# Seven products of halves for both feed-forward output projections of a hybrid attention and mLSTM model

## The chip, the cores and the metric

The kernel runs on one core of a Trainium2 chip. The metric is the device time of one execution in microseconds (us); the median of three runs is compared. A core has TensorE for matmuls (PE in the profile; PEld is its weight load), VectorE (DVE), ScalarE (ACT), GpSimd (POOL) and SyncE (SP), which issues most DMAs here. Matmuls write into PSUM, eight banks of 128 x 512 float32; the other operands lie in SBUF.

## The reference

Two layers over 512 tokens of width 1024, in float32: attention and a feed-forward, then an mLSTM and a feed-forward, then a last norm.

```python
h = x
for i in range(DEPTH):                      # 2
    if i % N_MIXERS == 0:
        h = h + dilated_attention_mixer(rms_norm(h, attn_norm[j]), ...)
    else:
        h = h + mlstm_mixer(rms_norm(h, mlstm_norm[j]), ...)
    h = h + swiglu(rms_norm(h, ffn_norm[i]), ffn_w_in[i], ffn_w_out[i])
return rms_norm(h, final_norm)

def swiglu(xn, w_in, w_out):                # D_FF = 2816
    gu = xn @ w_in
    return (silu(gu[..., :D_FF]) * gu[..., D_FF:]) @ w_out
```

The change concerns the last product, `hidden @ w_out`: 512 x 2816 by 2816 x 1024, once in each layer. The 2816 rows are 22 row tiles of 128.

## The kernel before

**Precision.** A float32 product is made of three matmuls in a faster 32-bit format (`SPLITS`): each operand is split into a high part (ACT copies it with rounding) and a low part (DVE subtracts the high part from the original), and high x high, high x low and low x high are summed in PSUM. `load_chunk` brings 512 KB of weights with SP into a ring of three buffers (`wraw`), `split_chunk` makes the parts in two further rings of three (`whi`, `wlo`). So a split runs at most two chunks ahead of PE.

**Order.** The code's order is a priority, not the order of execution: a planner in the framework fixes each engine's order ahead of time, by its own costs, and takes the first instruction in code order that is ready by its reckoning. So line 1561, far down in the mLSTM's code, runs on DVE at 845.38, among the norm that stands ahead of it. At run time each engine follows its fixed order and waits on semaphores. `defer(n, fn)` traces a function only n chunks of a projection later (`advance` counts them).

**Feed-forward input (`ffn_in`).** The hidden features come in pairs of row tiles, eleven tiles `hid[0..10]` of 128 x 2 x 512. The first six row tiles (`PLAIN`) are plain products; the rest are made in blocks of two as seven products of halves (the Strassen-Winograd scheme: `PRODUCTS`), with sums of weight halves and sums of token halves (T1 to T4) made on DVE. Each product is 24 matmuls of 256 columns. `prepare` splits the weights of the product two ahead.

**First layer's output projection.** `split_hidden` makes high and low parts of all of hid; then four `project` calls (tiles `fo`, matmuls in line 239) multiply feature-major: weights stationary, tokens moving, 512 columns. DVE adds the result to h in an order that interleaves the tokens (line 1287). Then `norm("mlstm", ...)`: high and low halves of h (lines 226, 227), squares (1007), sums of squares added up (1008), and, deferred by one chunk, a product with ones (1015) that gives each token's sum, a Newton root on DVE, diagonal tiles (323), and a product that broadcasts the result (329, `hook`). The mLSTM begins with `project_tokens_wide`, line 297: four chunks of two row tiles each, with the gates' product after the second.

**Second layer's output projection.** Token-major (tiles `fin`, line 1620): tokens stationary, weights moving. The two halves of the features are made one after the other, eight chunks, then three chunks tile by tile, so that the result tiles end in turn. h is transposed on PE (32 transposes, `residual`) and added; ACT squares the sum (1639), POOL multiplies it by the gain (1644), a short chain on small tiles gives the scale (1648 to 1655), ACT and DVE scale the halves, and they go out. The last tile is cut into two of 256 columns.

**The same scheme elsewhere.** The attention values are already made in seven products with 512 moving columns, and their weight sums are partly made by the DMA: a load issued from POOL with `accum_op=ALU.add` (line 606) adds to what lies in SBUF.

Of the kernel before, what the change touches and what calls it, by code (L numbers as in the profile page):

```python
# [17 lines left out]
P = 128  # L18
# [53 lines left out]
def tile_hybrid_dilated_attn_mlstm(  # L72
# [925 lines left out]
    def norm(key, k0, name):  # L998
# [21 lines left out]
        defer(1, sums)  # L1020
# [7 lines left out]
    def ffn_in(layer, fp, pair, rbc, hook, following):  # L1028
# [208 lines left out]
        out_weights = []  # L1237

        def prepare(n):
            if n < len(todo):  # L1240
                j, i = todo[n]
                if j not in prepared:
                    prepared[j] = weights_of(j)
                prepared[j][0][i]()
            else:
                out_weights.append(following(n - len(todo)))


        parts = [], []

        def split_hidden():
            i = len(parts[0])
            hi = fp.tile([P, 2, SEQ], F32R, tag="op%d" % (i + 1 if i else 0), name="f%dhh%d" % (layer, i))
            nc.scalar.activation(hi, hid[i], AF.Copy)
            lo = (place(i - 1, "hl", F32R) if i else
                  fp.tile([P, 2, SEQ], F32R, tag="op1", name="f%dhl" % layer))
            nc.vector.tensor_tensor(lo, hid[i], hi.bitcast(F32), op=ALU.subtract)  # L1257
            for part, x in zip(parts, (hi, lo)):
                part.append(x)
# [3 lines left out]
        for n, (j, i) in enumerate(todo):  # L1263
            prepare(n + AHEAD)
            if i == 0:
                steps_of = products(j, prepared[j][1])
            steps_of[i]()
            if i % 2:
                advance()
            if n >= len(todo) - 3:  # L1270
                split_hidden()
        while len(parts[0]) < len(hid):
            split_hidden()
        return [[tiles[k // 2][:, k % 2] for k in range(FC)] for tiles in parts], out_weights

    pair, rbc, _, hook = norm("ffn", 0, "n1")
    with ExitStack() as fctx:
        fp = pool(fctx, "ffn0")
        a, ready = ffn_in(0, fp, pair, rbc, hook,
                          lambda ch: split_chunk(weight_chunk(ffn_w_out[0], ch, 0, 4, "fo0_k%d" % ch)))  # L1280

        old, h = h, []

        def natural(c):
            def evac(m, acc):
                t = hp.tile([P, SEQ], F32, tag="h", name="hn%d" % (2 * c + m), bufs=KC + 1)
                nc.vector.tensor_tensor(t.rearrange("p (j c) -> p c j", c=4),
                                        acc.rearrange("p (c j) -> p c j", c=4),
                                        old[2 * c + m].rearrange("p (c j) -> p c j", c=4), op=ALU.add)
                h.append(t)  # L1290
            return evac
        for c in range(KC // 2):
            project(a, ffn_w_out[0], c * 256, FC, natural(c), "fo%d" % c, ready=ready)


    pair, rbc, rtok, hook = norm("mlstm", 0, "n2")
# [280 lines left out]
    with ExitStack() as fctx:  # L1577
# [3 lines left out]
        def load(ch, n):  # L1581
            src = wo[ch * 2 * P:(ch + 1) * 2 * P, n * 512:(n + 1) * 512].rearrange("(k p) n -> p k n", p=P)
            return split_weights(src, [P, 2, 512], "fw%d_%d" % (n, ch))
        a, ready = ffn_in(1, fp, pair, rbc, hook, lambda ch: load(ch, 0))
        gbc = fp.tile([P, D], F32, tag="t1", name="gbc")
        nc.gpsimd.dma_start(gbc, final_norm.unsqueeze(0).to_broadcast([P, D]))

        ht = [[None, None] for _ in range(TB)]
        ht_tiles = [fp.tile([P, 4, SEQ], F32, tag="w8", name="ht%d" % i, bufs=2) for i in range(2)]

        def residual(i):
            tb, n = i // 2, i % 2
            tp = ps.tile([P, 512], F32, tag="so"[i % 2], name="hT%d" % i, bufs=2)
            for k in range(4):
                transpose_into(tp, k, h[4 * n + k][:, tb * P:(tb + 1) * P])
            t = ht_tiles[i // 4][:, i % 4]
            nc.scalar.activation(t, tp, AF.Copy)
            ht[tb][n] = t
        NCH = FC // 2
        fss = fp.tile([P, TB, 3], F32, name="fss")  # L1600
        fpre, fv, fr, fa = (fp.tile([P, TB], F32, name="f" + n) for n in ("pre", "v", "r", "a"))
        nc.gpsimd.memset(fss, 0.0)
        nc.gpsimd.tensor_scalar(gbc, gbc, -0.5, None, op0=ALU.mult)
        tail = 3
        for n in range(2):
            acc = ([acc_tile("fin%d" % i) for i in range(3)] + [ps.tile([P, 512], F32, tag="t", name="fin3", bufs=1)]
                   if n == 0 else
                   [ps.tile([P, 512], F32, tag=tg, name="fin4", bufs=2) for tg in ("s", "s", "o", "o")]
                   + [acc_tile("fin5")])


            tiles = [(tb, tb, slice(0, 512)) for tb in range(TB)]
            if n == 1:
                tiles[-1:] = [(TB - 1, TB - 1, slice(0, 256)), (TB, TB - 1, slice(256, 512))]

            def mm(whl, ch, i, tb, cs):
                for k in range(2):
                    kk = 2 * ch + k
                    for a_, b_ in SPLITS:
                        nc.tensor.matmul(acc[i][:, cs], a[a_][kk][:, tb * P:(tb + 1) * P], whl[b_][:, k, cs],  # L1620
                                         start=(kk == 0 and (a_, b_) == SPLITS[0]),
                                         stop=(kk == FC - 1 and (a_, b_) == SPLITS[-1]))

            for ch in range(NCH - tail):
                whl = ready.pop(0) if ready else load(ch, n)
                for t in tiles:
                    mm(whl, ch, *t)
                if n == 0 and 1 <= ch <= TB:
                    residual(2 * ch - 2)
                    residual(2 * ch - 1)  # L1630
            last = [load(ch, n) for ch in range(NCH - tail, NCH)]
            for at, tb, cs in tiles:
                for i in range(tail):
                    mm(last[i], NCH - tail + i, at, tb, cs)
                t = ht[tb][n][:, cs]
                nc.vector.tensor_tensor(t, acc[at][:, cs], t, op=ALU.add)
                junk = npl.tile([P, SEQ], F32, tag="sq", name="fsq", bufs=2)
                part = 0 if n == 0 else 1 if cs.stop < 512 else 2
                nc.scalar.activation(junk[:, cs], t, AF.Square, accum_out=fss[:, tb, part:part + 1])
                if part == (1 if tb == TB - 1 else 0):  # L1640
                    nc.vector.tensor_tensor(fpre[:, tb:tb + 1], fss[:, tb, 0:1], fss[:, tb, 1:2], op=ALU.add)
                    nc.vector.tensor_scalar(fpre[:, tb:tb + 1], fpre[:, tb:tb + 1], 1.0 / D, EPS,
                                            op0=ALU.mult, op1=ALU.add)
                nc.gpsimd.tensor_tensor(t, t, gbc[:, n * 512 + cs.start:n * 512 + cs.stop], op=ALU.mult)
                if n == 1 and cs.stop == 512:

                    v = fv[:, tb:tb + 1]
# [37 lines left out]
```

## Time and profile before

| what | value |
|---|---|
| median of three runs | 1433.47 us (1430.98 to 1434.05) |
| profiled execution, its own time | 1431.08 us |
| its span, mean granted clock | 1428.8 us, 0.997 |
| PE busy | 1410.0 us, 7968 matmuls |
| DVE, ACT, POOL busy | 988.5, 621.3, 78.1 us |
| first output projection, first matmul to the first of the next stage | 724.98 to 844.69 us |
| second output projection, first to last matmul's start | 1294.51 to 1418.77 us |

Times in the profile count from the span's start. Busy time of PE overlaps from one matmul to the next, so a stage on PE is read from starts, not from durations. In rows of the profile an instruction stands with its line, the tile that it writes, the tiles that it reads and its shape; the name behind `<-` in brackets is what ended the idle time before it.

### The profile page before, as it was taken

How to read it: one execution, taken by the hardware profiler on the slowest of the kernel's cores; microseconds unless marked ns; L12 is line 12 of the kernel's file. 1: busy time of each engine (PE TensorE's matmuls, PEld its weight loads, DVE VectorE, ACT ScalarE, POOL GpSimd, SP SyncE). 2: the span in 40 equal slices, each digit the busy share in tenths (PEclk: the TensorE clock that was granted, in tenths of full speed). 3: DMA queues.
4: the chain of work that ended last, by engine and by line, in shares of the span. 5: the costliest groups of instructions: out<-in, count | busy, mean ns of one | idle time of the engine just before them, and what ended most of it. 6: DMA issues, size and time to landing. Idle time of an engine off the chain costs nothing. (4 is left out here: it accounts for less than half of the span.)

```text
span 1428.8 us, 20252 instructions
## 1 busy us (share of the span) xinstructions
PE 1410.0 (99%) x7968; PEld 1234.9 (86%) x7968; DVE 988.5 (69%) x1697; ACT 621.3 (43%) x1027; POOL 78.1 (5%) x131
## 2 busy tenths in 40 slices
PE   9999999999999999999999999999999999999997
PEld 7788888888888888999988888798888899998886
DVE  7976685966676587777863359987759777786223
ACT  7245522324224443454542234785544344555222
POOL 1014010100001000000000010100000000000101
PEclk9999999999999999999999999999999999999998
DMA  9538353363525333332233333221233233313231
GB/s 297 144 86 210 96 167 121 99 211 98 176 89 165 108 95 111 119 118 80 70 111 97 103 91 89 75 75 50 84 102 101 93 118 119 105 59 119 74 118 59
DMA packets 132182, 160.74 MB, mean 112 GB/s; under 512 B 7092, under 2 KB 112884, under 8 KB 132088
## 3 DMA queue, kind: packets, MB, share of 16 engines
q1 hardware_dynamic: 123696, 135.75, 30.7%
q0 software_dynamic: 6736, 22.59, 6.1%
q8 instruction: 62, 1.02, 0.3%
q10 hardware_dynamic: 1656, 1.12, 0.2%
q14 instruction: 32, 0.26, 0.1%
HBM read 145.28 MB, written 12.06 MB: 110 GB/s over the span
## 5 line engine op out<-in xcount | busy, mean ns | idle before, releaser
L1620 PE MATMUL fin<-fw_h,f1hh 128*128 128x512 f32 (+1 forms) x198 | 72.8, 368 | 0.0
L1620 PE MATMUL fin<-fw_l,f1hh 128*128 128x512 f32 (+1 forms) x198 | 72.5, 366 | 0.0
L1620 PE MATMUL fin<-fw_h,f1hl 128*128 128x512 f32 (+1 forms) x198 | 72.4, 366 | 0.0
L209 DVE TENSOR_TENSOR fw_l<-fw_w,fw_h 128x1024 fp32r<-128x1024 f32 x22 | 27.0, 1233 | 65.5 <-ACT fw_h L208 65.5
L209 DVE TENSOR_TENSOR fo_k_l<-fo_k_w,fo_k_h 128x1024 fp32r<-128x1024 f32 (+1 forms) x24 | 27.2, 1133 | 62.0 <-ACT fo_k_h L208 62.0
L239 PE MATMUL fo<-f0hh,fo_k_h 128*128 128x512 f32 x176 | 68.5, 389 | 0.0
L239 PE MATMUL fo<-f0hl,fo_k_h 128*128 128x512 f32 x176 | 68.5, 389 | 0.0
L239 PE MATMUL fo<-f0hh,fo_k_l 128*128 128x512 f32 x176 | 68.5, 389 | 0.0
L208 ACT ACTIVATE fo_k_h<-fo_k_w 128x1024 fp32r<-128x1024 f32 (+1 forms) x24 | 23.7, 989 | 74.4 <-PE fo L239 74.4
L208 ACT ACTIVATE fw_h<-fw_w 128x1024 fp32r<-128x1024 f32 x22 | 23.3, 1059 | 67.8 <-PE fin L1620 67.8
L1620 PEld LDWEIGHTS fin<-fw_h,f1hl 128*128 128x128 f32 x198 | 37.3, 189 | 6.1
L1620 PEld LDWEIGHTS fin<-fw_l,f1hh 128*128 128x128 f32 x198 | 37.4, 189 | 6.0 <-DVE fw_l L209 0.2
L1620 PEld LDWEIGHTS fin<-fw_h,f1hh 128*128 128x128 f32 x198 | 37.4, 189 | 6.0
L239 PEld LDWEIGHTS fo<-f0hh,fo_k_h 128*128 128x128 f32 x176 | 33.0, 188 | 6.9
L239 PEld LDWEIGHTS fo<-f0hl,fo_k_h 128*128 128x128 f32 x176 | 33.0, 188 | 6.9
L239 PEld LDWEIGHTS fo<-f0hh,fo_k_l 128*128 128x128 f32 x176 | 33.0, 188 | 6.7
L239 PE MATMUL f1j<-n_h,f1j_h 128*128 128x512 f32 x96 | 37.5, 390 | 0.0
L239 PE MATMUL f0j<-n_h,f0j_h 128*128 128x512 f32 x96 | 37.5, 390 | 0.0
L239 PE MATMUL f0j<-n_h,f0j_l 128*128 128x512 f32 x96 | 37.4, 389 | 0.0
L239 PE MATMUL f1j<-n_h,f1j_l 128*128 128x512 f32 x96 | 37.4, 389 | 0.0
L239 PE MATMUL f0j<-n_l,f0j_h 128*128 128x512 f32 x96 | 37.3, 389 | 0.0
L239 PE MATMUL f1j<-n_l,f1j_h 128*128 128x512 f32 x96 | 37.3, 389 | 0.0
(2127 smaller groups left out, 4896.8 us busy)
## 6 DMA issues: line engine op xcount, KB each, us to landing
f0j_w<-in_ffn_w_in_dram SPq DMA_DIRECT2D x28, 512.0 KB, 4.8
f1j_w<-in_ffn_w_in_dram SPq DMA_DIRECT2D x28, 512.0 KB, 3.6
fw_w<-in_ffn_w_out_dram SPq DMA_DIRECT2D x22, 512.0 KB, 3.9
fo_k_w<-in_ffn_w_out_dram SPq DMA_DIRECT2D x20, 512.0 KB, 3.4
awo_k_w<-in_attn_w_out_dram SPq DMA_DIRECT2D x8, 512.0 KB, 4.5
mv_k_w<-in_mlstm_w_in_dram SPq DMA_DIRECT2D x8, 512.0 KB, 3.6
mqk_k_w<-in_mlstm_w_in_dram SPq DMA_DIRECT2D x8, 512.0 KB, 3.8
mo_k_w<-in_mlstm_w_in_dram SPq DMA_DIRECT2D x8, 512.0 KB, 3.6
```

The lines of the kernel that those rows point to most:

```text
L208: nc.scalar.activation(hi[:, :n], raw[:, :n], AF.Copy)
L209: nc.vector.tensor_tensor(lo[:, :n], raw[:, :n], hi[:, :n].bitcast(F32), op=ALU.subtract)
L239: nc.tensor.matmul(acc, whl[a][:, k, m * P:(m + 1) * P], pairs[b][kk], start=(kk == 0 and (a, b) == SPLITS[0]), stop=(kk == nk - 1 and (a, ...
L1620: nc.tensor.matmul(acc[i][:, cs], a[a_][kk][:, tb * P:(tb + 1) * P], whl[b_][:, k, cs], start=(kk == 0 and (a_, b_) == SPLITS[0]), stop=(k ...
```

## The change

Sixteen of the 22 row tiles, as a matrix of 2 x 2 halves (rows 0 to 1023 and 1024 to 2047, columns 0 to 511 and 512 to 1023; tokens 0 to 255 and 256 to 511), become one unit of seven products; the last six row tiles stay plain. Class `Halves` runs it as 34 items in the order of `HALF_ORDER`: a11 (items 0 to 3), a12 (4 to 7), plain steps for the first half of the features p0 (8 to 10), s1 (11 to 14), s2 (15 to 18), p1 (19 to 21), s3 (22 to 25), s4 (26 to 29), a22 (30 to 33). A product's item has two row tiles of weights, 512 columns. Weight sums lie in four tiles "own" (a21 + a22; then, with a11 added on DVE, for s2; then with a12, for s4) and four tiles "first" (a11, then a11 + a21, for s3). What a load can add is added by accumulating DMAs from POOL; DVE adds four times. Token forms: B11 and B21 from `hid`, sums T1 to T4 made in place in `hid`, B22; their high and low parts lie in three slots of op tiles, written anew as products end (`HALF_SLOT`). Results lie in pairs of PSUM banks: c (a11, a12), u (a copy of a11's result, then s2, s3, a22), p (s1, s4); they are folded into h, or into the result tile, after each product.

In the first layer weights stay stationary and 256 tokens move; h is reordered afterwards by ACT (`natural`). In the second layer tokens are stationary and 512 weight columns move. The mLSTM's norm defers its sums by two chunks. `split_hidden` and the old projections go.

```diff
-    def norm(key, k0, name):
+    def norm(key, k0, name, wait=1):
...
-        defer(1, sums)
+        defer(wait, sums)
...
-        def split_hidden():
...
+            unit.early(n - len(todo) + len(PRODUCTS))
+
+    HALF_ORDER = (("a11", "B11"), ("a12", "B21"), ("p0", None), ("s1", "T1"), ("s2", "T2"), ("p1", None),
+                  ("s3", "T3"), ("s4", "B22"), ("a22", "T4"))
+    HALF_SLOT = {"B11": 0, "B21": 1, "T1": 2, "T2": 0, "T3": 1, "B22": 2, "T4": 0}
+
+    class Halves:
...
+        def load(self, to, col, ch, add=False):
+            view = to.rearrange("p (k n) -> p k n", k=2)
+            if add:
+                nc.gpsimd.dma_start(view, self.source(col, ch), accum_op=ALU.add)
+            else:
+                nc.sync.dma_start(view, self.source(col, ch))
+
+        def load_own(self, c):
+            p, tag = (self.fp, ("op12", "op13", "t1")[c]) if c < 3 else (xp, "x7")
+            self.own[c] = p.tile([P, 1024], F32, tag=tag, name="o%down%d" % (self.layer, c))
+            self.load(self.own[c], 1, c)
+            self.load(self.own[c], 1, 4 + c, True)
...
+        def prepare(self, n):
...
+            if place:
+                raw = wp.tile([P, 1024], F32, tag="wraw", name=nm + "_w", bufs=W_BUFS)
+                self.load(raw, place[0], place[1] + c)
+            else:
+                raw = self.first[c // 2][:, c % 2] if key == "s3" else self.own[c]
+            self.made[n] = split_chunk((raw, 1024, lambda t: t.rearrange("p (k n) -> p k n", k=2), nm))
+            if key == "s2":
+                self.load(self.own[c], 0, 4 + c, True)
+            if n + 2 < len(self.items) and self.items[n + 2][0] == "s2":
+                c2 = self.items[n + 2][2]
+                first = self.first[c2 // 2][:, c2 % 2]
+                nc.vector.tensor_tensor(self.own[c2], self.own[c2], first, op=ALU.add)
+                self.load(first, 1, c2, True)
...
+        EARLY = {2: (("B11", 0),), 3: (("B11", 1),), 4: (("B11", 2),), 5: (("B11", 3),), 6: (("B21", 0), ("B21", 1))}
+        STEPS = {0: (("B21", 2),), 1: (("B21", 3), ("plain", 8)), 2: (("plain", 9),), 3: (("plain", 10),),
+                 4: (("T1", 0),), 5: (("T1", 1),), 6: (("T1", 2),), 7: (("T1", 3),),
+                 8: (("T2", 0), ("T2", 1)), 9: (("T2", 2), ("T2", 3)), 10: (("T3", 0),), 11: (("T3", 1),),
+                 13: (("T3", 2),), 15: (("T3", 3),), 16: (("B22", 0),), 17: (("B22", 1),),
+                 19: (("B22", 2), ("B22", 3)), 20: (("T4", 0), ("T4", 1)), 21: (("T4", 2), ("T4", 3))}
...
+            for n, (key, okey, c) in enumerate(self.items):
+                self.prepare(n + 2)
+                if n < 4:
+                    self.load_own(n) if n < 3 else None
+                elif n == 4:
+                    self.load_own(3)
+                if 5 <= n < 9:
+                    self.load_first(n - 5)
+                for what, i in self.STEPS.get(n, ()):
+                    self.step(what, i)
...
+        def mul(dst, m, okey, c, whl, first, last):
+            for k in range(2):
+                for a, b in SPLITS:
+                    nc.tensor.matmul(dst[m // 2][:, (m % 2) * HALF:(m % 2 + 1) * HALF], whl[a][:, k, m * P:(m + 1) * P],
+                                     unit.form(okey, b, 2 * c + k),
...
+                whole[n] = [unit.bank(*b) for b in ((("acc", 3), ("t", 1), ("s", 2), ("s", 2)),
+                                                    (("acc", 3), ("acc", 3), ("acc", 3), ("t", 1)))[n]]
...
+        def natural(f):
+            t = hp.tile([P, SEQ], F32, tag="h", name="hn%d" % f, bufs=KC + 1)
+            nc.scalar.activation(t.rearrange("p (j c) -> p c j", c=4), h[f].rearrange("p (c j) -> p c j", c=4), AF.Copy)
+            h[f] = t
...
+    pair, rbc, rtok, hook = norm("mlstm", 0, "n2", 2)
...
+        def finish(tb, n):
+            t = ht[tb][n]
+            junk = npl.tile([P, SEQ], F32, tag="sq", name="fsq", bufs=2)
+            nc.scalar.activation(junk, t, AF.Square, accum_out=fss[:, tb, n:n + 1])
+            nc.gpsimd.tensor_tensor(t, t, gbc[n], op=ALU.mult)
...
+        def mul(dst, t, okey, c, whl, first, last):
+            for k in range(2):
+                for a, b in SPLITS:
+                    nc.tensor.matmul(dst[t], unit.form(okey, a, 2 * c + k)[:, t * P:(t + 1) * P], whl[b][:, k],
...
+        def after(banks, key, t):
+            if key == "s1":
+                fold(2 + t, 1, banks["p"][t], ALU.subtract)
+            elif key == "s2":
+                fold(2 + t, 0, banks["u"][t])
+            elif key == "s3":
+                fold(2 + t, 1, banks["u"][t], ALU.subtract)
+                finish(2 + t, 1)
+            elif key == "s4":
+                fold(2 + t, 0, banks["p"][t])
+                finish(2 + t, 0)
+            elif key == "a22":
+                fold(t, 1, banks["u"][t], ALU.subtract)
+                finish(t, 1)
+        unit.run((2, mul, mul_plain, after), also)
```

More of the change, by code (lines that the diff above doesn't have):

```diff
@@ L1245, in prepare @@
             else:
-                out_weights.append(following(n - len(todo)))
-        parts = [], []
-        def split_hidden():
[L1252 to L1259, printed above, removed]
+                unit.prepare(n - len(todo))
         for n in range(AHEAD):
@@ L1292, in tile_hybrid_dilated_attn_mlstm @@
-        for c in range(KC // 2):
-            project(a, ffn_w_out[0], c * 256, FC, natural(c), "fo%d" % c, ready=ready)
-    pair, rbc, rtok, hook = norm("mlstm", 0, "n2")
+        unit = Halves(0, fp, ffn_w_out[0])
+        ffn_in(0, fp, pair, rbc, hook, unit)
+        whole = {}
+        def mul(dst, m, okey, c, whl, first, last):
[3 more added lines that the diff above has]
+                                     unit.form(okey, b, 2 * c + k),
+                                     start=(first and m % 2 == 0 and k == 0 and (a, b) == SPLITS[0]),
+                                     stop=(last and m % 2 == 1 and k == 1 and (a, b) == SPLITS[-1]), skip_group_check=True)
@@ new lines, in mul_plain @@
+        def mul_plain(banks, key, c, whl, fresh, last):
+            n = int(key[1])
+            if fresh:
+                whole[n] = [unit.bank(*b) for b in ((("acc", 3), ("t", 1), ("s", 2), ("s", 2)),
+                                                    (("acc", 3), ("acc", 3), ("acc", 3), ("t", 1)))[n]]
+            for m in range(4):
+                for k in range(2):
+                    for a, b in SPLITS:
+                        nc.tensor.matmul(whole[n][m], whl[a][:, k, m * P:(m + 1) * P], unit.plain[c][b][k],
+                                         start=(fresh and k == 0 and (a, b) == SPLITS[0]),
+                                         stop=(last and k == 1 and (a, b) == SPLITS[-1]))
+                if last:
+                    f = 4 * n + m
+                    nc.vector.tensor_tensor(h[f], whole[n][m], h[f], op=ALU.add)
+                    if n == 0:
+                        fold(banks["c"], m, f, 0, ALU.add)
@@ L1297, in tile_hybrid_dilated_attn_mlstm @@
+        unit.run((4, mul, mul_plain, after))
+    pair, rbc, rtok, hook = norm("mlstm", 0, "n2", 2)
     w_in2 = mlstm_w_in[0]
@@ L1579, in tile_hybrid_dilated_attn_mlstm @@
         wo = ffn_w_out[1]
[L1581 to L1586, printed above, removed]
+        unit = Halves(1, fp, wo)
+        ffn_in(1, fp, pair, rbc, hook, unit)
@@ L1597, in residual, with gains_in @@
             nc.scalar.activation(t, tp, AF.Copy)
-            ht[tb][n] = t
-        NCH = FC // 2
-        fss = fp.tile([P, TB, 3], F32, name="fss")
+        def gains_in():
+            for n in range(2):
+                t = hp.tile([P, SEQ], F32, tag="h", name="gbc%d" % n, bufs=KC + 1)
+                nc.gpsimd.dma_start(t, final_norm[n * 512:(n + 1) * 512].unsqueeze(0).to_broadcast([P, 512]))
+                nc.gpsimd.tensor_scalar(t, t, -0.5, None, op0=ALU.mult)
+                gbc.append(t)
@@ L1601, in tile_hybrid_dilated_attn_mlstm, with also @@
+        def also(n):
+            if n < 4:
+                for i in (2 * n, 2 * n + 1):
+                    residual(i % TB, i // TB)
+            elif n == 6:
+                gains_in()
+        fss = fp.tile([P, TB, 2], F32, name="fss")
         fpre, fv, fr, fa = (fp.tile([P, TB], F32, name="f" + n) for n in ("pre", "v", "r", "a"))
         nc.gpsimd.memset(fss, 0.0)
[L1603 to L1616, printed above, removed]
-                for k in range(2):
[L1618 to L1647, printed above, removed]
-                    nc.vector.scalar_tensor_tensor(v, fss[:, tb, 2:3], 1.0 / D, fpre[:, tb:tb + 1],
-                                                   op0=ALU.mult, op1=ALU.add)
-                    r = fr[:, tb:tb + 1]
-                    a2 = fa[:, tb:tb + 1]
-                    nc.scalar.activation(r, v, AF.Sqrt)
-                    nc.vector.reciprocal(r, r)
-                    nc.vector.tensor_scalar(a2, r, v, r, op0=ALU.mult, op1=ALU.mult)
-                    nc.vector.scalar_tensor_tensor(r, a2, -3.0, r, op0=ALU.add, op1=ALU.mult)
-                    t0, t1 = ht[tb]
-                    nc.scalar.activation(t0, t0, AF.Copy, scale=r)
-                    nc.scalar.dma_start(out[tb * P:(tb + 1) * P, 0:512], t0)
-                    nc.vector.tensor_scalar(t1, t1, r, None, op0=ALU.mult)
-                    nc.sync.dma_start(out[tb * P:(tb + 1) * P, 512:1024], t1)
```

181 lines of the change are left out of this document (158 added, 23 removed).

## The prediction

> **What bounds the kernel now.** I read the page's busy shares first, then busy time by stage, then the matmuls' starts at the borders of the stages that change.
>
> ```profile
> span 1428.8 us, 20252 instructions
> ...
> PE 1410.0 (99%) x7968; PEld 1234.9 (86%) x7968; DVE 988.5 (69%) x1697; ACT 621.3 (43%) x1027; POOL 78.1 (5%) x131
> ```
>
> TensorE is busy for 99% of the span. The same by stage (columns: length; busy time and count of PE, PEld, DVE, ACT, POOL; clock; DMA share; GB/s):
>
> ```profile
> 100.00:110.00 10.00, 10.00 (x46) 8.24 (x45) 6.05 (x6) 4.83 (x6) 1.47 (x3) 1.00 0.80 227
> 563.00:725.00 162.00, 162.00 (x1349) 161.85 (x1348) 128.81 (x124) 86.73 (x105) 0.00 (x0) 1.00 0.30 93
> 725.00:845.00 120.00, 120.00 (x532) 99.39 (x531) 47.95 (x50) 33.39 (x39) 0.31 (x1) 1.00 0.32 100
> 905.00:915.00 10.00, 8.20 (x37) 6.26 (x36) 9.67 (x16) 7.56 (x23) 1.04 (x2) 1.00 0.00 0
> 1294.00:1419.00 125.00, 125.00 (x632) 106.24 (x630) 42.96 (x60) 37.22 (x54) 9.92 (x8) 1.00 0.28 89
> ```
>
> The second and third rows are the first layer's feed-forward input and output, the last one the second layer's output projection. In all three PE is busy from end to end at full clock, so an output projection is worth what its matmuls take, one start after another. The second row matters most for what follows: there DVE carries 128.81 of 162.00 us, and PE loses nothing. The fourth row, early in the mLSTM stage, is the counterexample: DVE at 9.67 of 10 us, and PE lost 1.8.
>
> A matmul's busy time overlaps its neighbours', so its price is the distance between starts:
>
> ```profile
> 699.90 0.28 PE L1186 MATMUL f0j_p<-f0B22l,f0j18S_h 128*128 128x256 f32 x1
> 700.02 0.28 PE L1186 MATMUL f0j_p<-f0B22h,f0j18S_l 128*128 128x256 f32 x1
> ...
> 724.98 0.40 PE L239 MATMUL fo<-f0hh,fo_k_h 128*128 128x512 f32 x1
> ...
> 844.69 0.39 PE L297 MATMUL mv<-mv_k_h,n_h 128*128 128x512 f32 x1
> ...
> 1294.51 0.40 PE L1620 MATMUL fin<-fw_h,f1hh 128*128 128x512 f32 x1
> ```
>
> With 256 moving columns (the input's seven products) starts are 0.12 us apart. The first output projection runs from 724.98 to 844.69, 119.71 us for 3 x 176 = 528 matmuls of 512 columns: 0.2267 each. Two matmuls of 256 cost 0.24: halving the moving side loses 6%.
>
> ```profile
> L1620 PE MATMUL fin<-fw_h,f1hh 128*128 128x512 f32 x154 | 60.4, 392 | 0.0
> ...
> L209 DVE TENSOR_TENSOR fw_l<-fw_w,fw_h 128x1024 fp32r<-128x1024 f32 x22 | 27.0, 1233 | 65.5 <-ACT fw_h L208 65.5
> ...
> L1620 PE MATMUL fin<-fw_h,f1hh 128*128 128x256 f32 x44 | 12.4, 282 | 0.0
> ```
>
> These three rows, of the second output projection, give three kinds of matmul each: 462 of 512 columns and 132 of 256. It runs from 1294.51 to 1418.77 + 0.12 = 1418.89 (that start is quoted with the tail below): 124.4 us. 462 x 0.2267 + 132 x 0.12 = 120.6; the 3.8 left are its 32 transposes.
>
> **The matmuls after.** Sixteen of 22 row tiles become seven products of halves (8 row tiles, 256 tokens, 512 features), the other six stay plain.
> First projection, feature-major: 7 x 4 feature tiles x 8 row tiles x 3 = 672 matmuls of 256 columns, 80.6 us, and 8 x 6 x 3 = 144 of 512, 32.6 us: 113.3 against 119.7, so -6.4.
> Second, token-major: 7 x 2 token tiles x 8 x 3 = 336 of 512 columns, plus the same 144: 480 x 0.2267 = 108.8, with the transposes 112.6 against 124.4: -11.8. It gains more since it keeps 512 columns, and its last tile is no longer split.
> Together -18.2 us.
> [...]
>
> **VectorE.** By the weight-split row (1.23 us for 1024 columns) and 0.69 for 512 and 0.42 for 256 (tail rows below), a unit costs: 34 weight splits 41.8; 28 low halves of token forms 19.3; 16 sums of forms 11.0; 4 weight sums 4.9; three plain tiles 3.7; folds 15.6 in the first unit (8 x 0.69, 24 x 0.42) and 12.4 in the second (18 x 0.69). That is 96.3 and 93.1; six forms and two splits (6.6) are done in the last input products. So 90 of 113 us and 87 of 113, against 47.95 and 42.96 now (eleven token splits and 24 or 22 weight splits go), and near the 80% of the second quoted row. The average is covered; the peak is items 8 to 14 (last plain step of the first half, both sum products). There DVE has 29.4 us of work in the first unit (7 splits 8.6, 4 sums 4.9, three T3 forms 4.1, four T2 forms 5.5, folds 4.4 + 1.7) against 3 x 5.44 + 4 x 2.88 = 27.8 of PE. Two splits stand ahead of PE in the three-deep ring. If DVE keeps the written order, the excess of 1.6 and seven waits for ACT's high half (0.63 each, the 512-column ACT row below) make up to 6.0 us of stall. But the order is a planner's, which takes what is ready: T1 forms need only slots freed in the last input products, T2 forms only B11's, free after item 3. With T2 ahead the peak is 23.9, and nothing waits. Bounds per unit 0 and 6; I take 1.0, nearer to the second quoted row than to the fourth: +2.0 for both.
>
> **PSUM.** s1 in the first unit takes the two banks that the last plain step fills last. It waits for one add of 0.69 after the third tile, and the fourth tile's matmuls (1.36) cover that: 0, at most the folds ahead of it on DVE, inside the 6 above. The copy of a11 into the u banks (0.63) has half an item, 1.4, of cover.
>
> **GpSimd and DMA.** Per unit 38 loads of 512 KB, 19.9 MB in 113 us, is 176 GB/s; now it is 100 and 89. The attention values, which run the same seven products with the same accumulating loads, reach 227 at a share of 0.80 with PE at 10.00 of 10 (first row above). All twelve accumulations go through POOL's queue, behind loads on SP's. "first" and the third "own" tile lie where buffers free up during the input products (share 0.30); the first two "own" tiles must wait for the last one, the fourth for the last plain split. The first user of "own" is prepared eight products later, over 20 us. I cost this at 0; if that cover is gone it is the third rival. In the second unit POOL also multiplies eight result tiles by the gain while DVE works:
>
> ```profile
> 1284.85 3.04 POOL L1603 TENSOR_SCALAR gbc<-gbc 128x1024 f32<-128x1024 f32 x1 [3.24 <-DMA gbc<-in_final_norm_dram]
> ...
> 1285.16 2.06 DVE L209 TENSOR_TENSOR f1j20S_l<-f1j20A,f1j20S_h 128x1024 fp32r<-128x1024 f32 x1
> ```
>
> A DVE subtraction beside a POOL instruction took 2.06 instead of 1.23: +0.83. Two such multiplies fall into the peak: 1.7 us of DVE work, inside the bounds.
> [...]
>
> **The mLSTM's start.** Feature tiles 4 to 7 of h now end with the last item, and the norm's sums are put off by two chunks instead of one.
>
> ```profile
> 850.13 0.95 PE L1015 MATMUL n2ss<-ones,n2ssum 128*128 128x1 f32 x8
> ...
> 851.11 0.16 DVE L1017 COPY n2v<-n2ss 128x4 f32<-128x4 f32 x1 [0.32 <-PE n2ss L1015]
> ...
> 854.99 1.66 DVE L323 TENSOR_SCALAR n2dg<-cst,n2rhl 128x128 fp32r<-128x128 f32 x8
> ```
>
> Now the sums run 5.44 us after the first mLSTM matmul (844.69), the statistics reach DVE 0.98 later, and the diagonal tiles are done at 856.65, 5.54 after that. After: sums at 10.88, statistics at 11.86, tiles at 16.2 to 17.4 (without or with the weight split that sits among them); PE, through sums (0.8) and 16 gate matmuls (3.6), is ready for them at 15.3. So PE, and the gate chain on DVE, lose 0.9 to 2.1: I take 1.5. The lower bound is 0, if PE runs the next chunk first; the upper one is a rival. The high and low halves of tiles 0 to 3 are ready before the last item, those of 4 to 7 are needed 10.9 us later: 0. ACT's reordering copy of h has no row here; between the plain 0.63 and twice that, eight of them take 5 to 10 us, spread over the last eight items.
>
> **The tail.** The last matmul feeds a fold, a square, a short chain and a scaling:
>
> ```profile
> 1414.78 0.69 DVE L1636 TENSOR_TENSOR ht<-fin,ht 128x512 f32<-128x512 f32 x1 [0.51 <-PE fin L1620]
> ...
> 1415.50 0.63 ACT L1639 ACTIVATE fsq<-ht 128x512 f32<-128x512 f32 x1 [1.01 <-DVE ht L1636]
> ...
> 1416.31 1.30 POOL L1644 TENSOR_TENSOR ht<-ht,gbc 128x512 f32<-128x512 f32 x1 [2.65 <-ACT fsq L1639]
> ...
> 1418.77 0.28 PE L1620 MATMUL fin<-fw_h,f1hl 128*128 128x256 f32 x1
> 1419.09 0.42 DVE L1636 TENSOR_TENSOR ht<-fin,ht 128x256 f32<-128x256 f32 x1 [0.62 <-PE fin L1620]
> 1419.55 0.42 ACT L1639 ACTIVATE fsq<-ht 128x256 f32<-128x256 f32 x1 [0.89 <-DVE ht L1636]
> ...
> 1421.28 0.72 ACT L1657 ACTIVATE ht<-ht,fr 128x512 f32<-128x512 f32 x1 [0.79 <-DVE fr L1655]
> ```
>
> The last tile is 512 wide instead of 256: fold 0.69 for 0.42, +0.27. Now scaling starts 1.73 after the square. After, POOL's multiply starts 0.81 behind it and takes 1.30: 2.11 and a semaphore, so +0.4. Together +0.7, at least 0.3, at most 1.5 if the tile before is still in the queues.
>
> **Sum.** -18.2 + 2.0 + 1.5 + 0.7 = -14.0 us on a profiled execution of 1431.1 (span 1428.8): 1417.1. The median shown is 1433.5, 2.4 above it, so 1419.5.
>
> **Rivals.**
> 1. VectorE's order binds: the planner's order leaves DVE waiting in the peak. For: the fourth window row. Against: the second. Two units at their bound of 6 are +12 for 2.0: 1429.5; half of that is as likely, so about 1427.
> 2. The handover: planned times differ from real ones, and ACT and DVE do the norm only behind the last product. Then the first mLSTM chunk waits for a fold 0.42, a copy, a high half (0.63 each) and a low half 0.69, 2.4, later tiles at 1.3 each, and the gate chain moves by some 6: +7 in place of 1.5, 1425. Against it: PE has no gap at 844.69 now, with tiles ending as late.
> 3. Slower: weight loads queue behind the unit's own tiles on SP. By item 10 a unit needs 8 raw, 8 own and 4 first loads, 10.5 MB; at 227 GB/s that is 46 us, where PE comes there after 33. If none starts before the unit, each stalls 13: +26, 1445. It decides from some 18 us of late loads on. Against it: only 0.30 of the DMA time is taken in the input products before.
> 4. The products do not cost as the rows say, for example the 512-column token form slows down with its operands: nothing in the attention values' row speaks for it.
>
> **How the numbers follow.** Forecast 0.62, by its own bounds 1416 to 1423; rival 1 0.17, rival 2 0.08, rival 3 0.08, the rest, better or worse, 0.05. The range leaves out rival 3 and the worst of rival 1: 1415 to 1428. A difference under 0.2%, 2.9 us, is what a measurement of this kernel cannot tell from none. Faster is all but rival 3 and a part of the rest: 0.88; same 0.04; slower 0.08.
>
> **What would show it.** Right: matmul starts of the first projection from first to last 113 to 115 us, of the second 112 to 115; DVE near 80% in both; DMA near 180 GB/s; the mLSTM's broadcast at some 17 us after its first matmul. Wrong: PE waits for weight low halves in items 10 to 18 (rival 1), a gap before the first mLSTM matmul (rival 2), ACT's splits released by DMA (rival 3).

## The result and the profile after

The changed kernel takes 1422.88 us (median of six runs, 1422.22 to 1423.83) against 1432.36 (six runs, the three known before among them, 1430.98 to 1434.05): ratio 0.9934, 95% interval 0.9922 to 0.9947, so some 9.5 us less. Forecast were 14.0 less, 1419.5. The profiled execution took 1423.79, 0.9 above its median, where the one of before lay 1.3 below the median of its six runs; by the two profiles alone the gain is 7.3.

The first two lines of the page of after:

```profile
span 1422.0 us, 20903 instructions
...
PE 1399.3 (98%) x8142; PEld 1233.0 (87%) x8142; DVE 1072.7 (75%) x1832; ACT 669.5 (47%) x1099; POOL 110.3 (8%) x158
```

TensorE has 174 more matmuls than before and is busy 10.7 us less (1410.0 before). The starts at the borders of the stages, PE's timeline of after:

```profile
725.47 0.40 PE L1436 MATMUL o_acc<-o0B,o0a_h 128*128 128x256 f32 x2
...
842.99 0.63 PE L297 MATMUL mv<-mv_k_h,n_h 128*128 128x512 f32 x2
...
845.46 0.28 PE L1436 MATMUL o_o<-o0T,o0a_l 128*128 128x256 f32 x1
...
1299.15 0.40 PE L1823 MATMUL o_acc<-o1a_h,o1B 128*128 128x512 f32 x1
...
1413.84 0.39 PE L1823 MATMUL o_o<-o1a_h,o1T 128*128 128x512 f32 x1
```

The first projection runs from 725.47 to 845.46 + 0.12, and five matmuls of the mLSTM (1.13 us) lie inside. The second one's first and last starts are the other two rows. With the starts of before, which the prediction quotes, and the end of the last transfer (the last quarter microsecond in which a DMA moved, 1424.3 and 1420.8):

| stage | before | after | difference | forecast |
|---|---|---|---|---|
| start of the first projection | 724.98 | 725.47 | +0.5 | 0 |
| first projection | 119.7 | 119.0 | -0.7 | -5.4 |
| to the second projection's first matmul | 449.8 | 454.7 | +4.9 | +1.5 |
| second projection, first to last start | 124.3 | 114.7 | -9.6 | -10.8 |
| last start to the end of the last transfer | 5.5 | 7.0 | +1.4 | +0.7 |
| from there to the span's end | 4.5 | 1.2 | -3.3 | 0 |
| sum | | | -6.8 | -14.0 |

So the second projection brought nearly what was forecast, the first one next to nothing, and the mLSTM's start took 3.4 us more than forecast. The last line of the table is hardly the change's: in the twelve experiments it is 1.2 to 2.5, and 2.2 where the second projection is the old one.

Where PE stood still, from the list of waits of after (total, times, longest):

```profile
PE o_acc L1436 <- ACT o_o L1423: 2.0, 2, 1.1
...
PE n2ss L1015 <- DVE n2ssum L1008: 1.2, 1, 1.2
...
PE o_o L1436 <- DVE o0a_l L209: 0.7, 1, 0.7
PE o_o L1436 <- DVE hx L1460: 0.6, 1, 0.6
PE o_acc L1836 <- DVE o1p_l L209: 0.6, 1, 0.6
PE mv L297 <- DVE mv_k_l L209: 0.5, 1, 0.5
```

Busy time by stretch, with the columns of the prediction's table (PE, PEld, DVE, ACT, POOL; clock; DMA share; GB/s):

```profile
735.00:745.00 10.00, 8.02 (x65) 7.61 (x65) 7.92 (x12) 4.67 (x7) 2.37 (x2) 1.00 1.03 252
725.00:845.00 120.00, 116.53 (x823) 108.71 (x822) 87.55 (x116) 60.46 (x75) 13.16 (x11) 1.00 0.59 145
1299.00:1414.00 115.00, 113.98 (x515) 93.08 (x513) 83.48 (x110) 57.93 (x84) 29.00 (x24) 1.00 0.58 149
830.00:840.00 10.00, 9.28 (x78) 9.08 (x76) 6.95 (x11) 9.94 (x14) 0.00 (x0) 1.00 0.46 129
840.00:850.00 10.00, 9.38 (x56) 7.93 (x54) 8.72 (x16) 9.74 (x14) 3.63 (x13) 1.00 0.40 110
854.00:856.00 2.00, 1.78 (x4) 1.49 (x5) 1.97 (x9) 0.00 (x0) 0.00 (x0) 0.50 0.30 44
```

PE is not full in the first projection (116.53 of 120), where it was before. DVE carries 73% of either unit. ACT is at 9.94 and 9.74 of 10 us at the end of the first one, and behind that TensorE's granted clock falls to 0.50.

**The copies.** ACT's timeline around the copies of a11's result (L1423):

```profile
736.13 1.06 ACT L208 ACTIVATE o0a_h<-o0a_w 128x1024 fp32r<-128x1024 f32 x1 [1.54 <-DMA o0a_w<-in_ffn_w_out_dram]
...
737.61 0.58 ACT L1423 ACTIVATE o_o<-o_acc 128x512 f32<-128x512 f32 x1
739.34 1.06 ACT L208 ACTIVATE o0a_h<-o0a_w 128x1024 fp32r<-128x1024 f32 x1 [1.15 <-DMA o0a_w<-in_ffn_w_out_dram]
740.30 0.58 ACT L1423 ACTIVATE o_o<-o_acc 128x512 f32<-128x512 f32 x1
```

Each copy stands behind a weight split that waited for its load (1.54 and 1.15 us). PE had finished a11, and stood 1.1 and 0.9 us for them.

**The mLSTM's start.** All engines, after the first chunk of the mLSTM:

```profile
849.74 0.61 ACT L1007 ACTIVATE n2sq<-hn 128x512 f32<-128x512 f32 x1
...
850.26 1.99 ACT L208 ACTIVATE mv_k_h<-mv_k_w 128x1024 fp32r<-128x1024 f32 x2
...
851.30 1.05 PE L1015 MATMUL n2ss<-ones,n2ssum 128*128 128x1 f32 x8 [1.23 <-DVE n2ssum L1008]
...
852.39 0.16 DVE L1017 COPY n2v<-n2ss 128x4 f32<-128x4 f32 x1 [0.43 <-PE n2ss L1015]
...
852.94 1.23 DVE L209 TENSOR_TENSOR mv_k_l<-mv_k_w,mv_k_h 128x1024 fp32r<-128x1024 f32 x1
...
854.22 0.79 PE L297 MATMUL mv<-mv_k_l,n_h 128*128 128x512 f32 x1 [0.53 <-DVE mv_k_l L209]
...
854.81 0.63 PE L297 MATMUL mv<-mv_k_h,n_l 128*128 128x512 f32 x1
...
855.24 0.63 PE L297 MATMUL mv<-mv_k_h,n_h 128*128 128x512 f32 x1
```

ACT makes the last tile's square (849.74) and only then the high half of the second chunk's weights (850.26). PE waits 1.23 us for the sums, does the four products that need no low half, and waits again for the low half. The low half stands behind two orders: on ACT its high half comes after the last tile, and on DVE it comes only after the first steps on the sums' result (n2v, 852.39), which had to wait for PE. From 854.81 on matmuls of 512 columns are 0.43 us apart instead of 0.227. That is the half clock, until 859.5: some 2.5 us lost in all. With the gaps before it (1.6 around the sums, 1.1 before the low half) that is 5.2; the whole stage lost 4.9.

### The profile page after: what moved, and what is told of

It reads as the page before. It is cut to its first block, busy times and chain, and to the rows that moved or that the text cites. A ratio compares the mean times of both kernels' runs of the same rounds, so it can differ in the third digit from the quotient of the medians.

```text
span 1422.0 us, 20903 instructions
## 1 busy us (share of the span) xinstructions
PE 1399.3 (98%) x8142; PEld 1233.0 (87%) x8142; DVE 1072.7 (75%) x1832; ACT 669.5 (47%) x1099; POOL 110.3 (8%) x158
## 3 DMA queue, kind: packets, MB, share of 16 engines
q8 instruction: 64, 1.05, 0.3%
## 4 chain that ended last, share of the span: by engine, by line
PE 78%; DVE 13%; DMA 4%; ACT 3%; issue 2%; POOL 0%; ACTq 0%; DVEq 0%; POOLq 0%
PE f1j L239 5%; PE f0j L239 5%; PE f1j_u L1186 4%; PE f0j_u L1186 4%; PE mwo L239 3%; PE f1j_c L1186 3%; PE f0j_c L1186 3%; PE f1j_p L1186 3%; PE f0j_p L1186 3%; PE o_o L1823 2%; PE v_o L664 2%; PE o_acc L1836 2%; PE awo L239 2%; PE mo L239 2%; PE o_o L1436 2%
## 5 line engine op out<-in xcount | busy, mean ns | idle before, releaser
L524 DVE TENSOR_TENSOR rot<-rot,sinr 32x1024 f32<-32x1024 f32 x24 | 28.9, 1205 | 0.0
L239 PE MATMUL mo<-n_h,mo_k_h 128*128 128x512 f32 x64 | 25.4, 396 | 0.0
L239 PE MATMUL mo<-n_l,mo_k_h 128*128 128x512 f32 x64 | 25.2, 394 | 0.0
L239 PE MATMUL mo<-n_h,mo_k_l 128*128 128x512 f32 x64 | 25.2, 394 | 0.0
L239 PE MATMUL mqk<-n_h,mqk_k_h 128*128 128x512 f32 x64 | 25.1, 392 | 0.0
L239 PE MATMUL awo<-ao_h,awo_k_h 128*128 128x512 f32 x64 | 25.1, 392 | 0.0
L239 PE MATMUL mqk<-n_h,mqk_k_l 128*128 128x512 f32 x64 | 25.0, 391 | 0.0
L239 PE MATMUL mqk<-n_l,mqk_k_h 128*128 128x512 f32 x64 | 25.0, 390 | 0.0
L239 PE MATMUL awo<-ao_h,awo_k_l 128*128 128x512 f32 x64 | 24.9, 390 | 0.0
L239 PE MATMUL mwo<-yo_l,mwo_k_h 128*128 128x512 f32 x64 | 24.9, 389 | 0.0
```

The costliest lines, as they stand in the source:

```text
L239: nc.tensor.matmul(acc, whl[a][:, k, m * P:(m + 1) * P], pairs[b][kk], start=(kk == 0 and (a, b) == SPLITS[0]), stop=(kk == nk - 1 and (a, ...
L524: nc.vector.tensor_tensor(sh, sh, sinr.unsqueeze(1).to_broadcast([R, 2, SEQ]), op=ALU.mult)
```

## The experiments

All are timed in five rounds against the kernel before, whose median lay between 1431.24 and 1432.59. A ratio of 0.001 is 1.4 us. Stages are read as above, from one profile each. Whether TensorE's clock fell in that one execution is in them: in the six profiles that have the mLSTM code of after, the mLSTM stage takes 454.7 to 455.3 us where the clock was at half for 6.8 us and 452.9 to 453.7 where it was for 3.4 (the last section has more on this).

| run | ratio (95%) | median | first projection | mLSTM stage | second |
|---|---|---|---|---|---|
| after | 0.9934 (0.9922 to 0.9947) | 1422.88 | 119.0 | 454.7 | 114.7 |
| second projection alone | 0.9915 (0.9902 to 0.9929) | 1419.41 | 119.7 | 449.4 | 113.4 |
| first projection alone | 1.0011 (1.0002 to 1.0020) | 1433.51 | 118.6 | 455.3 | 124.3 |
| copies on DVE | 0.9938 (0.9924 to 0.9951) | 1422.97 | 119.1 | 453.5 | 114.9 |
| "own" loaded later | 0.9933 (0.9920 to 0.9945) | 1423.36 | 118.9 | 454.7 | 114.9 |
| "first" loaded later | 0.9943 (0.9931 to 0.9955) | 1424.24 | 118.6 | 453.7 | 115.2 |
| p0 between a11 and a12 | 0.9919 (0.9906 to 0.9932) | 1420.60 | 115.9 | 452.9 | 114.8 |
| h reordered in halves | 0.9924 (0.9912 to 0.9936) | 1421.31 | 117.1 | 452.8 | 114.9 |
| gates after three chunks | 0.9965 (0.9953 to 0.9976) | 1427.78 | 119.2 | 458.9 | 114.5 |
| p0 between, halves | 0.9914 (0.9900 to 0.9927) | 1418.75 | 115.1 | 451.4 | 114.4 |
| the same, sums behind the gates | 0.9926 (0.9914 to 0.9938) | 1420.80 | 115.1 | 455.6 | 115.0 |
| p0 between, halves, split first | 0.9885 (0.9871 to 0.9898) | 1414.91 | 115.1 | 450.1 | 115.0 |
| split first alone | 0.9921 (0.9908 to 0.9935) | 1420.26 | 118.5 | 450.0 | 115.1 |

**One projection at a time.** The old code of one layer beside the new code of the other.

> First projection and the norm's delay as before, second projection as after. Theory (the traces' stages: the second projection takes 9.3 us less, the end 2.0 us less, while the first projection's 0.7 us and more are given back in the mLSTM's start): the second projection alone brings 11 us, 1421 us, faster than the whole change. Rival (both projections bring what the forecast said, only everything somewhat smaller): this half brings some 6 to 7 of the 9.5 us, 1426 us. In both cases the mLSTM's start looks as before: sums 5.4 us after its first matmul, no clock under 1.00 there.

> First projection and the norm's delay as after, second projection as before. Theory: the first projection gains 0.7 us and the mLSTM's start loses 4.9, with a stretch of clock 0.50 behind the norm's sums, so 1 to 5 us slower than before: 1434 to 1437 us. Rival: it brings its share of the gain, 3 us, 1429 us.

The theory held for both, in sign and place. The second projection alone brings 12.2 us (0.9915 of 1432), by the medians more than the whole change, though the intervals just meet; the first alone makes the kernel slower, by 1.6 us, a little less than the theory's range. That loss goes with the clock: of the eleven executions, the four with a mean granted clock of 0.998 took 1431.5 to 1432.4 us, as the kernel before does, and the seven with 0.996 or 0.997 took 1433.2 to 1434.9. Its list of waits and its clock show the mLSTM's start of after again:

```profile
PE n2ss L1015 <- DVE n2ssum L1008: 1.2, 1, 1.2
...
PE mv L297 <- DVE mv_k_l L209: 0.8, 1, 0.8
```

```profile
854.00:856.00 2.00, 1.90 (x5) 1.53 (x6) 1.93 (x10) 0.00 (x0) 0.00 (x0) 0.50 0.31 65
```

**Whose fault are the copies?** Three runs on the cause, one on the cover. The edits in short:

```diff
-nc.scalar.activation(banks["u"][t], banks["c"][t], AF.Copy)
+nc.vector.tensor_copy(banks["u"][t], banks["c"][t])            # copies on DVE
-load_own in items 0, 1, 2, 4
+load_own in items 4, 5, 6, 7                                   # "own" later
-load_first in items 5 to 8
+with tc.issue_after(last_on_pe()): load_first in items 8 to 11 # "first" later
-order a11, a12, p0, s1, ...; T1's first form in item 4
+order a11, p0, a12, s1, ... (first layer); plain forms in items 0 to 2, B21's last in 3 and 4
```

> As after, but the two copies of a11's result (both layers) are made by VectorE and not ScalarE. Theory (the copies stand on ScalarE behind weight splits that wait for their loads; PE stands 2.0 us in the first unit): those PE waits go, 2 us less than after in the first unit, 1420.5 to 1421.5 us. Rival (VectorE's own order is as late, it too waits for the splits): the wait changes its releaser from ACT to DVE and the time stays at 1423 us.

The rival held: the wait changes its releaser, and the time stays.

```profile
PE o_acc L1436 <- DVE o_o L1423: 1.3, 1, 1.3
```

> As after, but the four tiles own are loaded in items 4 to 7 instead of 0, 1, 2 and 4 (both layers); ScalarE's order around the copies is the same. Theory (loads of own, and the accumulations behind them, crowd the weight loads of a11 and a12 and make them late): ScalarE's splits in items 2 to 8 wait less for DMA, the copies start earlier, PE's 2.0 us at the copies shrink to under 1, 1421 to 1422 us; danger: s1 waits for own. Rival (the copies are late by ScalarE's written order alone): 1423 us, with the same 2.0 us of PE wait at the copies.

The rival's time came, and PE stood 1.6 us at the copies instead of 2.0. But this does not show the rival's reason alone: ACT's split ahead of the second copy, which follows at 739.41, still waits for DMA, so the edit did not make the loads come in time.

```profile
738.45 1.06 ACT L208 ACTIVATE o0a_h<-o0a_w 128x1024 fp32r<-128x1024 f32 x1 [1.56 <-DMA o0a_w<-in_ffn_w_out_dram]
```

> As after, but the four tiles first are loaded from item 8 on, behind PE's work of item 7, in both layers, 2 MB out of the crowded stretch 715 to 755 us. Theory (the DMA engines are full there, share 0.93 to 1.03, so weight loads come late, splits and copies behind them): the DMA share falls below 0.9 in items 0 to 8, ScalarE's splits wait less for DMA, PE's 2.0 us at the copies shrink to under 1, 1421 to 1422 us. Rival (the accumulations are what fills the engines, and ScalarE's order decides): 1423 us, PE still stands about 2 us at the copies.

Here the loads do come earlier in the profile. The waits of ACT for a11's and a12's loads fall from 6.4 to 3.3 us, PE's at the copies from 2.0 to 0.7; ACT's list of waits of after and of this run for 724 to 760, and PE's of this run:

```profile
ACT o0a_h L208 <- DMA o0a_w<-in_ffn_w_out_dram: 6.4, 4, 3.2
ACT o0p_h L208 <- DMA o0p_w<-in_ffn_w_out_dram: 4.1, 3, 2.5
```

```profile
ACT o0a_h L208 <- DMA o0a_w<-in_ffn_w_out_dram: 3.3, 3, 1.3
```

```profile
PE o_acc L1437 <- ACT o_o L1424: 0.7, 2, 0.5
PE o_acc L1450 <- DVE o0p_l L209: 0.5, 1, 0.5
```

So PE stood less where the loads came earlier. That this edit made them earlier is not shown: in the last run below, whose first projection has the code of after, PE stood only 0.3 us at the copies too, and ACT's split ahead of the second copy did not wait at all. The DMA share, which the theory had falling, stayed (1.04 for 735 to 745). The time did not follow either, it cannot be told from that of after: the stage gains 0.4 us only, as a plain step waits for a low half instead (0.5), and in the second projection another wait for a low half comes on top (0.6).

> As after, but in the first layer the plain steps p0 stand between a11 and a12, so that the copies of a11's result have 16 us of cover instead of 1.4. Theory (the copies are late by what stands ahead of them on ScalarE, and nothing else is late in the same items): PE's 2.0 us there go, 2 us less than after, 1420.5 to 1421.5 us. Rival (the weight loads are late as such): PE waits at another place of the same items, for a split of p0 or a12, and the time stays at 1422.5 to 1423.5 us.

The theory held in the stage: the first projection takes 115.9 instead of 119.0, and PE's list of waits has no row for 720 to 800. The time is 2.1 us less than after's by the ratios, as the theory has it, but the two intervals overlap. ACT's splits wait for DMA as long as ever:

```profile
ACT o0a_h L208 <- DMA o0a_w<-in_ffn_w_out_dram: 7.7, 4, 2.9
ACT o0p_h L208 <- DMA o0p_w<-in_ffn_w_out_dram: 4.0, 3, 1.6
```

So it is neither the queue nor the loads as such that cost: of 11.7 us of waiting on ACT, PE feels only what stands ahead of an instruction without cover. Shown, by the stage: with 16 us of cover the loss is gone.

**What delays the mLSTM?**

```diff
-nc.scalar.activation(<all of h reordered>, h[f], AF.Copy)      # after the fold, 128x512
+nc.scalar.activation(<final half reordered>, h[f] half, AF.Copy)
+nc.vector.tensor_tensor(<other half reordered>, h[f] half, bank, op)   # the last fold itself
```

> As after, but h is reordered in halves: ScalarE copies only the token half that is already final, and VectorE's last fold writes the other half straight into the reordered tile. Theory (ScalarE is full before the mLSTM, 9.94 and 9.74 of 10 us, eight reordering copies of 1.14 us among its work; the squares, the sums and the weight split come late for that, PE stands 1.4 + 1.1 us and the clock falls to 0.50 behind it): ScalarE has some 4.5 us less to do, PE's waits at the sums and at the weight split fall below 1 us together, the clock stays at 1.00, 1418 to 1420 us. Rival (the sums are late because the last product's tiles end late, whoever reorders): the waits and the clock stay, 1422 to 1423.5 us.

In between, and in time not to be told from after; this profile also lost 2.5 us ahead of the first projection, at a place that the change does not touch (last section). PE's waits at the sums and the split went from 1.2 + 0.5 to 0.5 + 1.0, and the clock fell all the same. The first projection gained 1.9 us: the last product's own waits (0.7 and 0.6 of after) shrank to 0.2, the copies' from 2.0 to 1.0.

```diff
-norm("mlstm", 0, "n2", 2); first_values((0, 1)); gates(); hook()
+norm("mlstm", 0, "n2", 3); first_values((0, 1, 2)); gates(); hook()
```

> As after, but the norm's sums are put off by three chunks of the mLSTM's first product, and the gates' product and the broadcast follow the third chunk. Theory (the loss is PE's standing still at the sums and the clock that follows; the gate chain has slack): no wait at the sums, the clock stays at 1.00, 3 to 4 us less than after, 1419 to 1420 us. Rival (the gate chain behind the broadcast has no slack): it starts some 5 us later, the stretch 900 to 920 us loses what the start gains, 1422 to 1426 us.

The rival's time and more. Moreover the edit missed its mark: `defer` sets a priority, and the planner put the sums where they had been, between the second chunk's high and low products; PE waited 1.2 us there as before. Only the gate chain came later, and the clock fell a second time, at 911 (mean granted clock of this profile 0.995, of after 0.997).

The next run has both edits that shortened a stage, p0 between a11 and a12 and h in halves.

> Both edits that shortened the first half together: p0 between a11 and a12 in the first layer, and h reordered in halves. Theory (two separate losses, one at the copies, one on ScalarE before the mLSTM): the stages add, first projection 116 us or less, mLSTM 452.5 us, 1418.5 to 1419.5 us. Rival (with the unit faster, the mLSTM's start only waits longer for the same squares and weight splits): no better than the first edit alone, 1420.5 us.

The stages came as the theory has them, 115.1 and 451.4. The clock stayed at 1.00 in the mLSTM's start of this profile, where the run with h in halves had 3.4 us at half, as an estimate 1.7 us lost (half of 3.4), where 1.4 lie between their mLSTM stages. In time the run cannot be told from the first edit alone (0.9914 and 0.9919).

```diff
-defer(wait, sums)                       # sums when the planner has room
+first_values((0, 1)); gates(); run(sums); first_values((2,)); hook()
```

> As the run with both edits, but the norm's sums are tied behind the gates' product (so that the order of TensorE really has them there), and the broadcast follows the third chunk. Theory (PE stands at the sums because the fixed order has them ahead of the second chunk's products; the clock falls behind that): no wait at the sums, and with under 1 us of standing the clock stays at 1.00; mLSTM stage 450 to 451 us, 1416 to 1417.5 us. Rival (what PE waits for is the second chunk's weight split on ScalarE, so the wait and the clock only move there): waits of 1 us and more and a stretch at 0.50 stay, and the gate chain comes later: same time or up to 3 us more than the run with both edits.

The rival held, except that the clock stayed at 1.00. The sums cost nothing now, and PE's list of waits shows what stood behind them, the second chunk's low half, and later the price of the late gate chain:

```profile
PE mv L297 <- DVE mv_k_l L209: 2.5, 1, 2.5
PE mqk L239 <- DVE mqk_k_l L209: 2.5, 3, 2.0
```

What is left is the order on ACT: the last tile's norm ahead of the second chunk's split. The last two runs change that, one on top of the two edits, one alone.

```diff
+def mv_weights(): ...   # load and split one chunk of the mLSTM's first product
-norm("mlstm", 0, "n2", 2)
+norm("mlstm", 0, "n2", 2, {4: mv_weights, 6: mv_weights})   # called ahead of tiles 4 and 6
```

> Both edits as before (p0 between a11 and a12, h reordered in halves), and the splits of the mLSTM's first two weight chunks stand ahead of the norm's last two tiles in the code, so that ScalarE makes the second chunk's high half as soon as the unit frees its buffer; TensorE's order then has the whole second chunk ahead of the sums. Theory (ScalarE's order, last tile's norm ahead of the second chunk's weight split, is what TensorE waits for): waits at the weight split and at the sums together under 0.5 us, mLSTM stage 449.5 to 450.5 us, no clock of 0.50 there, 1416 to 1417.5 us. Rival (the last tile's own fold, high half and square are the chain, and lose what the split gains): the wait moves to the gates' product or stays at the sums, 1418 to 1420 us.

> As after, with only the splits of the mLSTM's first two weight chunks moved ahead of the norm's last two tiles. Theory: the first projection stays at 119 us, the mLSTM stage falls from 454.7 to 451 us or less with no clock of 0.50, 1419 to 1420 us. Rival (the eight reordering copies of 1.14 us on ScalarE are the loss, whatever the order): the waits move to the gates or the sums, the stage stays at 453 us or more, 1421.5 to 1423 us.

The theory held in both, with 1414.91 below its range and 1420.26 just above. ACT's timeline of the run with the split alone, and its busy time with the clock:

```profile
846.04 1.05 ACT L208 ACTIVATE mv_k_h<-mv_k_w 128x1024 fp32r<-128x1024 f32 x1
846.99 1.13 ACT L1469 ACTIVATE hn<-hx 128x512 f32<-128x512 f32 x1
```

```profile
840.00:850.00 10.00, 9.91 (x57) 8.82 (x58) 8.55 (x15) 9.75 (x14) 3.62 (x13) 1.00 0.35 98
850.00:860.00 10.00, 10.00 (x49) 8.23 (x48) 8.07 (x27) 3.18 (x6) 0.00 (x0) 1.00 0.42 123
```

One instruction of 1.05 us, made at 846.04 instead of 850.26, and the order that the planner makes of it (the whole second chunk ahead of the sums) bring the mLSTM stage from 454.7 to 450.0, within 0.3 us of before, although the eight reordering copies still fill ACT. The time follows less than the stage, ratio 0.9921 against 0.9934, 1.9 us, which the intervals do not tell apart; its runs spread from 1417.80 to 1422.78, and what differs between them the one profile does not show.

With all three edits the kernel takes 1414.91 us, ratio 0.9885: 16.5 us less than before (0.0115 of 1432), and 7 less than the change as it was (0.0049), which the intervals do tell apart. Against the two edits without the split it gains more in time than in its stages: those add up to 680.2 us against 680.9, and 2.5 of the 3.2 us between the two profiles lie ahead of the first projection, where the other one's clock fell. So that the time came below its range is in part luck. The stretch behind the first chunk there:

```profile
850.00:860.00 10.00, 9.77 (x47) 7.87 (x46) 7.38 (x27) 2.12 (x2) 0.00 (x0) 1.00 0.33 105
```

## Why the prediction was right, and where it was not

**The matmuls: right.** Starts of 256-column matmuls stayed 0.12 apart, of 512-column ones 0.2267: one sum product of the second projection, 48 matmuls, runs from 1342.91 to 1353.79, 10.88 us. The 113.3 and 112.6 us would be what the units take where nothing waits; the second took 114.7 to its last start, the first came to 115.1 in the best runs. DVE's average was right too (73% in both units against some 80%), and the peak, rival 1, cost one wait of 0.6 us. (The sum for the peak has two slips, without effect: items 8 to 14 are the three plain steps and one sum product, not both, and a weight's high half takes ACT 1.06 us, not 0.63.)

**The copies: the step that failed first.** "The copy of a11 into the u banks (0.63) has half an item, 1.4, of cover." The copy took 0.58, but I counted from the matmul that frees it, not from its place in ACT's fixed order, and took the splits for ready. The DMA engines were full there (share 1.03 in the first row of the table by stretch), as I had not reckoned: my 180 GB/s were a mean over the unit, and the mean came to no more than 145 and 149 in the two. Rival 3's sign appeared, ACT's splits released by DMA, 6.4 + 4.1 us of it. Its price did not, except through the copies: 2.3 us. The last product's waits for a low half and a fold add 1.9, gaps of 0.1 to 0.3 the rest of the 5.7.

**The mLSTM's start: mis-sized, 4.9 for 1.5.** I reckoned when PE and the gate chain would be ready for each other, put the halves of the late tiles at "0", and gave ACT's copies no price. One took 1.14, near the upper end of what I had allowed, and eight of them with the norm's work filled ACT. The wait that bound was not named at all: the second chunk's weight split, whose buffer the last product holds to its end, stands in ACT's order behind the last tile's norm. Nor was the clock, whose fall is about half of the 4.9. The broadcast came at 865.12, 22 us after the mLSTM's first matmul (842.99), instead of 17. Rival 2 had the place right, the handover, with 7 us for 1.5, but its sign, a gap before the first mLSTM matmul, did not come: PE mixed the first chunk into the unit's end and paid one chunk later.

**The tail: +1.4 for +0.7**, within its bounds. Timeline of after:

```profile
1414.48 0.49 DVE L1817 TENSOR_SCALAR ht<-ht,fr 128x512 f32<-128x512 f32 x1
1414.88 0.68 DVE L1797 TENSOR_TENSOR ht<-ht,o_o 128x512 f32<-128x512 f32 x1
...
1415.60 0.63 ACT L1802 ACTIVATE fsq<-ht 128x512 f32<-128x512 f32 x1 [0.47 <-DVE ht L1797]
...
1417.71 0.72 ACT L1815 ACTIVATE ht<-ht,fr 128x512 f32<-128x512 f32 x1 [0.96 <-DVE fr L1813]
```

The tile before last still held DVE with its scaling (1414.48), the case that the upper bound was for, so the fold started 0.8 us after the last matmul instead of 0.2. From the square to the scaling it took 2.11 (1415.60 to 1417.71), as forecast.

The steps on TensorE and the tail came out 10.0 us short (4.7, 3.4, 1.2, 0.7). The end of the span gave 3.3 back, the medians lie 2.2 further apart than the two profiles, and its base, a median of three runs, was 1.1 above that of six. No step of the forecast contains these three. So the number came nearer, 3.4 us from the median, than its steps had earned: that is luck.

## What to carry to other kernels

Where a stage is made shorter, write down, for each engine that works in order, what stands in its queue around the two ends of the stage: here an instruction without cover inherited every wait ahead of it (2.0 us of TensorE at the copies), and a weight split behind a late tile stopped TensorE one chunk later (0.5 us, and 2.5 with the sums behind the gates). Try the parts of a change alone: here one half carried the gain and the other cost a little, until one instruction of ScalarE's order was moved. A deferral that only lowers a priority has to be looked up in the order that results.

## What was not expected of the hardware

**The clock after a short stop.** At a place that the change does not touch, PE waits for a transfer in every kernel here. In twelve of the fourteen profiles it stood 0.96 to 1.68 us, and the clock stayed at 1.00. In the two others, those with h reordered in halves and with that and p0 between, it stood 2.05 and 1.91 us, and the clock was at 0.50 for 3.4 us behind it; their first projections start at 727.98 and 727.65 instead of 725.47. PE's timeline of after, of the run with h reordered in halves, and the latter's clock:

```profile
466.09 1.83 PE L873 MATMUL a3o<-a3pT,v 128*128 128x128 f32 x14 [1.42 <-DMA a3pT<-a3pD]
```

```profile
467.00 2.40 PE L873 MATMUL a3o<-a3pT,v 128*128 128x128 f32 x14 [2.05 <-DMA a3pT<-a3pD]
```

```profile
468.00:470.00 2.00, 2.00 (x12) 2.00 (x11) 0.00 (x0) 0.00 (x0) 0.00 (x0) 0.52 0.90 326
```

With h in halves the half clock lasted from 468.08 to 471.48, by the clock of 0.52 above and 0.63 in the next two microseconds; at the mLSTM's start of after it lasted 6.83 us, from 852.91 to 859.74.

The length of one stop does not settle it. In the run with the sums behind the gates PE stood 2.5 us at the mLSTM's start and 2.0 us some 50 us later, and the clock stayed at 1.00 both times. At the mLSTM's start of after it stood 1.23 us ahead of the sums, and the clock fell 1.6 us after that stop's end (852.91), ahead of the end of the next one (0.53, up to 854.22). Two runs stood 0.5 us at the sums and 1.0 at the split alike: with h in halves the clock fell, with p0 between as well it stayed. No run varied the stop alone, so neither a limit nor what decides is shown. For a plan it means that a stop of 1 to 2 us can cost, as an estimate, 1.7 us more (half of 3.4), and need not.

**Accumulating loads.** For 720 to 770 of after the DMA queues show (packets, MB, share of the 16 engines' time), q0 with POOL's accumulating loads, q1 with the plain ones:

```profile
q1 hardware_dynamic: 4431, 8.53, 51.4%
q0 software_dynamic: 1444, 2.79, 32.9%
```

That is 11.8% for a megabyte against 6.0%. By bytes, as the prediction took them, the twelve accumulations of a unit looked like a third of its loads; in that stretch they took time like twice as many. Whether the adding costs it, or POOL's queue, is not separated here.
